# The second layer's Fourier projection, split into even and odd parts of its tokens and its channels

## Chip, core and metric

The kernel runs on one NeuronCore of one Trainium2 chip. The metric is the device time of one execution in microseconds (us). Three runs of the kernel before gave 2589.39, 2590.97 and 2591.15 us, so its median is 2590.97 us.

## What is computed

A two-layer encoder trunk over T = 272 tokens (16 meta tokens and 256 others) of width D = 2048, all in float32. Per layer:

```
h = RMSNorm(x)
[q | k | v | f | ga | gf] = h @ W_in
attention: 8 query heads, 2 key heads of 128, per-head RMSNorm, 2-D rotary, softmax over all 272 tokens
fourier:   for each of 8 groups of 128 channels of f: Re(FFT2 over tokens and channels), ortho
x = x + (sigmoid(ga) * (attn @ W_attn_br) + sigmoid(gf) * (fourier @ W_four)) @ W_out
x = x + W_down( silu(dwconv3(RMSNorm(x) @ W_up_gate)) * (RMSNorm(x) @ W_up_val) )
```

The real part of the 2-D transform is a cosine transform over tokens of a cosine transform over channels, less a sine transform of a sine transform. The cosine part sees only what is even in the tokens (x[n] + x[272-n]) and even in the channels (w[c] + w[128-c]), the sine part only what is odd in both.

## The kernel before

Everything is kept with channels on the 128 partitions and tokens along the free dimension. The residual stream XT is [128, 16, 272]; xH and xL are its two halves in fp32r after multiplication by the norm's weights (`norm_split`, L379), H the rounded value and L the rest. A product of two float32 numbers is three fp32r matmuls: H times H, H times L, L times H.

**Weights** are streamed in the order written down in the list `order` (from L117 on), in chunks of [128, 4, 256] float32 (512 KB). `advance` (L158) issues a chunk's load on SP's queue, four buffers deep (RAW = 4), and queues two tasks: for the weights of the Fourier branch, `fold_w` (L176), two VectorE instructions that make sums and differences of halves of the chunk (tile `wpm`); for every chunk `split_w` (L182), a ScalarE cast into `wh` and a VectorE subtraction into `wl` (three buffers each). `pump` (L169) issues these tasks between the matmuls, two chunks ahead (LOOK = 2).

**Groups.** `group` (L212) makes 256 output channels of one projection: over 16 input tiles it issues, for each of two halves m, the three matmuls of L240, L241 and L242 into one PSUM bank. Banks have two tags of four each, "mm" for the groups and "aux" for everything else. Where only 256 tokens are needed (the second layer's feed-forward), the first two matmuls become one of 512 columns (L236, L237). `four_group` (L256) does the same for the Fourier branch's output weights, on even and odd parts: one matmul of 276 columns (H and L of 138 tokens, L275), then one of 138 (L276).

**Side work** is written as generators: `push` puts one on the list `shadow`, and `step` (L197), called after every second of a chunk's eight weight tiles (four times a chunk, 16 times a group of four chunks), runs at most one that is due up to its next `yield n`, which makes it wait n steps. `drain` (L208) runs all of them to the end. What is written this way sets priorities; the framework's planner then fixes each engine's order of instructions at compile time, and lets an instruction that is ready in its plan pass one that is not. In the trace VectorE thus runs L847 of a second half ahead of L850 of the first.

**Order around the change.** Layer 0: f, k, v, four groups q, gates and branches, `o`, then the feed-forward: 22 pairs of groups `ug` and `uv` and 16 groups `d`, 264 chunks, with `norm_stats` (L397) at its start. Layer 1 begins with the four groups f (L553): each is 256 channels over all 272 tokens, `f_evac` (L449) multiplies by 1/rms and adds and subtracts mirrored tokens, and the generator `f_chan` (L463) makes the channel transform by float32 matmuls of 65 columns; after the fourth, `f_tok` (L498) makes the token transform. Then come k with `head_evac` and `kstats` (L607), v with `vtrans`, q with `q_stage` (L665), which releases `attend` (L692), the attention that runs beside the rest.

Of the kernel before, what the change touches and what calls it, by code (L numbers as in the profile page):

```python
# [10 lines left out]
F32 = mybir.dt.float32  # L11
F32R = mybir.dt.float32r
# [4 lines left out]
P = 128  # L17
# [17 lines left out]
FF_SPLIT = (24, 20)  # L35

# [66 lines left out]

def _rep(ap, n):
    return ap.unsqueeze(1).to_broadcast([ap.shape[0], n, ap.shape[1]])
# [3 lines left out]
def encoder_kernel(ctx, tc, xT, params, consts, bmat, w_in, w_abr, w_four, w_f64, w_out, w_up, w_down, outT):  # L109
# [3 lines left out]
    psum = ctx.enter_context(tc.tile_pool(name="psum", bufs=4, space=bass.MemoryType.PSUM))  # L113

# [3 lines left out]
    for l in range(DEPTH):  # L118
        def g(w, mg, k0, k1):
            return [(w[l, mg, c], CW) for c in range(k0 // CW, k1 // CW)]  # L120
        if l == 0:
            f01 = [g(w_in, IN_F + i, 0, KT) for i in range(2)]
            order.append(((l, "f01"), [ch for pr in zip(*f01) for ch in pr]))
        for i in range(2 if l == 0 else 0, 4):
            order.append(((l, "f", i), g(w_in, IN_F + i, 0, KT)))
# [270 lines left out]

    def norm_stats(holder):  # L397
# [26 lines left out]
    for l in range(DEPTH):  # L424
# [6 lines left out]
        with tc.tile_pool(name=f"mix{l}", bufs=1) as mp:  # L431
            E = mp.tile([P, NG, T], F32, tag="q1", name="E")
            AHn = 3 * 4 * T
            ALn = 2 * 4 * T
            o1Hf = mp.tile([P, AHn], F32R, tag="aH", name="o1H")
            o1Lf = mp.tile([P, ALn], F32R, tag="aL", name="o1L")
            o1H, o1L = (t_[:, :4 * 4 * HC].rearrange("p (i b c) -> p i b c", i=4, b=4) for t_ in (o1Hf, o1Lf))
# [4 lines left out]
            def rt(name):  # L442
                return mp.tile([P, 2, T], F32, tag="r", name=name, bufs=7)
# [18 lines left out]

            def f_chan(i):  # L463
# [6 lines left out]
                hh = o1H[:, i]  # L470
                nc.scalar.copy(hh, pv[:, :, 0:HC])
                nc.vector.tensor_tensor(o1L[:, i], pv[:, :, 0:HC], hh.bitcast(F32), op=ALU.subtract)
                for m in range(2):
                    h1 = o64[:, 0, 4 * m + i:4 * m + i + 1]
                    nc.scalar.copy(h1, pv[:, m, HC:HC1])
                    nc.vector.tensor_tensor(o64[:, 1, 4 * m + i:4 * m + i + 1], pv[:, m, HC:HC1], h1.bitcast(F32), op=ALU.subtract)
                if i == 3:
                    yield 1
# [16 lines left out]
                    yield from f_tok()  # L495
                yield 1

            def f_tok():  # L498
# [10 lines left out]
                for i in range(4):  # L509
                    pb = psum.tile([P, 512], F32, tag="aux", name="ps_fb")  # L510
                    pv = pb.rearrange("p (e n) -> p e n", e=2)[:, :, :TH]
                    for b in range(2):
                        oh, ol = (t_[:, i, 2 * b:2 * b + 2, :].rearrange("p m c -> p (m c)") for t_ in (o1H, o1L))
                        nc.tensor.matmul(pv[:, b, :], oh, BH[:, b, :], start=True, stop=False)
                        nc.tensor.matmul(pv[:, b, :], oh, BL[:, b, :], start=False, stop=False)
                        nc.tensor.matmul(pv[:, b, :], ol, BH[:, b, :], start=False, stop=False)
                        nc.tensor.matmul(pv[:, b, :], o1r[:, i, :], br3[:, b, :], start=False, stop=True)
                    nc.scalar.copy(fr[:, i, :, 0, :], pv)
                    nc.vector.tensor_tensor(fr[:, i, :, 1, :], pv, fr[:, i, :, 0, :].bitcast(F32), op=ALU.subtract)
                    yield 2  # L520

            if l == 0:
# [27 lines left out]
                nc.vector.tensor_scalar(bgh, prm[:, P_BG:P_BG + DEPTH * 2 * KT], 0.5, None, op0=ALU.mult)  # L550
            else:
# [47 lines left out]
            ps = group((l, "k", 0), xr(0), T)  # L599
            kp, ksq = head_evac(ps, prm[:, P_KN + l:P_KN + l + 1], "kp", 0)  # L600
# [6 lines left out]
            def kstats():  # L607
# [19 lines left out]
                rope(kp, qs, kH, kL)  # L627

            push(kstats(), 4)
# [9 lines left out]
            def vtrans():  # L639
                for kv in range(NKV):  # L640
# [12 lines left out]
                    yield 2  # L653

# [7 lines left out]
            qH = mp.tile([P, NH, T], F32R, tag="q1", name="qH")  # L662
            qL = mp.tile([P, NH, T], F32R, tag="q2", name="qL")
# [28 lines left out]
            def attend():  # L692
                for kv in range(NKV):
# [166 lines left out]
        with tc.tile_pool(name=f"ffn{l}", bufs=1) as fp:  # L860
            hold = {}
            push(norm_stats(hold), 8)
            fused = 2 * W2 <= 512
            k0 = 0
            for c, n in enumerate(FF_SPLIT):
                gHL = fp.tile([P, FF_SPLIT[0], 2, T], F32R, tag="gHL", name="gHL")
                gH, gL = gHL[:, :, 0, :], gHL[:, :, 1, :]
                for i in range(k0 // MG, (k0 + n) // MG):
                    ps = group((l, "ug", i), xr(lo), W)
                    drain()  # L870
# [45 lines left out]
                k0 += n  # L916

# [20 lines left out]

def _cols(a):
    return a.reshape(-1, P).T  # L940
# [27 lines left out]
```

## Time and profile before

| what | value |
|---|---|
| median of three runs | 2590.97 us |
| the profiled execution's own time | 2590.29 us |
| its span, first to last instruction | 2588.4 us |
| TensorE, share of the span | 100% (2577.4 us) |
| VectorE | 65% (1691.3 us) |
| ScalarE | 47% (1210.0 us) |
| DMA queue of SP | 457.37 MB, 51.6% of 16 engines |
| layer 1's groups f, first to last matmul | 1329.3 to 1380.9 us |
| layer 0's feed-forward, first ug to last d | 533.0 to 1329.2 us |

The profile is one execution. "Busy" is the share of the span in which an engine ran something; a matmul is pipelined and its end is modelled, so how fast TensorE gets on is read from the distance between the starts of two matmuls and not from their length. L numbers are lines of the kernel before. The clock granted to TensorE was 1.000 throughout.

### The profile page before, as it was taken

How to read it: one execution, taken by the hardware profiler on the slowest of the kernel's cores; microseconds unless marked ns; L12 is line 12 of the kernel's file. 1: busy time of each engine (PE TensorE's matmuls, PEld its weight loads, DVE VectorE, ACT ScalarE, POOL GpSimd, SP SyncE). 2: the span in 40 equal slices, each digit the busy share in tenths (PEclk: the TensorE clock that was granted, in tenths of full speed). 3: DMA queues.
4: the chain of work that ended last, by engine and by line, in shares of the span. 5: the costliest groups of instructions: out<-in, count | busy, mean ns of one | idle time of the engine just before them, and what ended most of it. 6: DMA issues, size and time to landing. Idle time of an engine off the chain costs nothing.

```text
span 2588.4 us, 47800 instructions
## 1 busy us (share of the span) xinstructions
PE 2577.4 (100%) x19706; PEld 2514.1 (97%) x19706; DVE 1691.3 (65%) x2689; ACT 1210.0 (47%) x1736; POOL 18.6 (1%) x38
## 2 busy tenths in 40 slices
PE   8999999999999999999999999999999999999999
PEld 8999999999999999999999999999999998899988
DVE  7687767766565445565556878677766665566654
ACT  5455434554444334444444555445544543354443
POOL 0000000000000000000000000000000000000000
PEclk9999999999999999999999999999999999999999
DMA  6544555545555555555544545555555555555554
GB/s 234 165 151 164 191 180 189 181 171 177 174 177 174 176 174 174 176 175 176 174 169 151 173 155 199 192 194 188 183 186 186 186 187 188 187 183 186 186 199 159
DMA packets 131995, 465.34 MB, mean 180 GB/s; under 512 B 15296, under 2 KB 19264, under 8 KB 131776
## 3 DMA queue, kind: packets, MB, share of 16 engines
q1 hardware_dynamic: 127408, 457.37, 51.6%
q10 hardware_dynamic: 4368, 4.92, 0.6%
q8 instruction: 154, 2.52, 0.4%
q14 instruction: 65, 0.53, 0.1%
HBM read 457.35 MB, written 2.10 MB: 178 GB/s over the span
## 4 chain that ended last, share of the span: by engine, by line
PE 97%; DVE 1%; DMA 1%; ACT 1%; issue 0%; SPq 0%; POOL 0%; DVEq 0%; ACTq 0%
PE ps_ug L241 7%; PE ps_ug L240 7%; PE ps_ug L242 7%; PE ps_uv L236 6%; PE ps_d L236 6%; PE ps_d L240 4%; PE ps_d L241 4%; PE ps_d L242 4%; PE ps_uv L240 3%; PE ps_uv L241 3%; PE ps_uv L242 3%; PE ps_uv L237 3%; PE ps_d L237 3%; PE ps_o L241 2%; PE ps_o L242 2%; PE ps_o L240 2%
## 5 line engine op out<-in xcount | busy, mean ns | idle before, releaser
L188 DVE TENSOR_TENSOR wl<-raw,wh 128x1024 fp32r<-128x1024 f32 (+1 forms) x834 | 1017.0, 1222 | 724.0 <-ACT wh L187 718.6
L187 ACT CAST wh<-raw 128x1024 fp32r<-128x1024 f32 (+1 forms) x834 | 871.6, 1047 | 1025.1 <-issue 168.7
L241 PE MATMUL ps_ug<-xHL,wh 128*128 128x272 f32 (+1 forms) x1408 | 402.4, 286 | 0.0
L240 PE MATMUL ps_ug<-xHL,wh 128*128 128x272 f32 (+1 forms) x1408 | 402.0, 285 | 0.0
L242 PE MATMUL ps_ug<-xHL,wl 128*128 128x272 f32 (+1 forms) x1408 | 401.8, 285 | 0.0
L240 PEld LDWEIGHTS ps_ug<-xHL,wh 128*128 128x128 f32 x1408 | 265.4, 188 | 1.0
L241 PEld LDWEIGHTS ps_ug<-xHL,wh 128*128 128x128 f32 x1408 | 265.5, 189 | 0.1
L242 PEld LDWEIGHTS ps_ug<-xHL,wl 128*128 128x128 f32 x1408 | 264.9, 188 | 0.0
L236 PE MATMUL ps_uv<-xHL,wh 128*128 128x512 f32 x704 | 247.7, 395 | 0.0
L236 PE MATMUL ps_d<-gHL,wh 128*128 128x512 f32 x664 | 233.1, 395 | 0.0
L241 PE MATMUL ps_d<-gHL,wh 128*128 128x272 f32 (+1 forms) x744 | 214.4, 288 | 0.0
L240 PE MATMUL ps_d<-gHL,wh 128*128 128x272 f32 (+1 forms) x744 | 214.1, 288 | 0.0
L242 PE MATMUL ps_d<-gHL,wl 128*128 128x272 f32 (+1 forms) x744 | 214.0, 288 | 0.0
L241 PE MATMUL ps_uv<-xHL,wh 128*128 128x272 f32 x704 | 203.1, 288 | 0.0
L240 PE MATMUL ps_uv<-xHL,wh 128*128 128x272 f32 x704 | 202.9, 288 | 0.0
L242 PE MATMUL ps_uv<-xHL,wl 128*128 128x272 f32 x704 | 202.7, 288 | 0.0
L237 PE MATMUL ps_uv<-xHL,wl 128*128 128x256 f32 x704 | 197.7, 281 | 0.0
L237 PE MATMUL ps_d<-gHL,wl 128*128 128x256 f32 x664 | 186.5, 281 | 0.0
L236 PEld LDWEIGHTS ps_uv<-xHL,wh 128*128 128x128 f32 x704 | 132.4, 188 | 29.9
L236 PEld LDWEIGHTS ps_d<-gHL,wh 128*128 128x128 f32 x664 | 125.0, 188 | 29.2
L240 PE MATMUL ps_ga<-xHL,wh 128*128 128x272 f32 (+1 forms) x512 | 148.2, 289 | 0.0
L240 PE MATMUL ps_gf<-xHL,wh 128*128 128x272 f32 (+1 forms) x512 | 147.1, 287 | 0.0
(273 smaller groups left out, 5899.6 us busy)
## 6 DMA issues: line engine op xcount, KB each, us to landing
raw<-in_w_up SPq DMA_DIRECT2D x352, 512.0 KB, 3.5
raw<-in_w_in SPq DMA_DIRECT2D x207, 512.0 KB, 3.6
raw<-in_w_down SPq DMA_DIRECT2D x176, 512.0 KB, 3.4
raw<-in_w_out SPq DMA_DIRECT2D x64, 512.0 KB, 3.5
raw<-in_w_four SPq DMA_DIRECT2D x32, 512.0 KB, 3.9
raw<-in_w_abr SPq DMA_DIRECT2D x32, 512.0 KB, 3.6
qs<-qp ACTq DMA_DIRECT2D x32, 68.0 KB, 3.8
outT<-ot ACTq DMA_DIRECT2D x16, 128.0 KB, 3.5
```

Of the source, the lines that this page charges most:

```text
L187: nc.scalar.copy(h[:, a:b], r[:, a:b])
L188: nc.vector.tensor_tensor(lo[:, a:b], r[:, a:b], h[:, a:b].bitcast(F32), op=ALU.subtract)
L236: nc.tensor.matmul(o2, h[:, c, sl], ab, start=kt == 0, stop=False)
L237: nc.tensor.matmul(o, lo[:, c, sl], ab[:, 0, :], start=False, stop=kt == nk - 1)
L240: nc.tensor.matmul(o, h[:, c, sl], a, start=kt == 0, stop=False)
L241: nc.tensor.matmul(o, h[:, c, sl], b, start=False, stop=False)
L242: nc.tensor.matmul(o, lo[:, c, sl], a, start=False, stop=kt == nk - 1)
```

## The change

Layer 1 no longer projects f from 272 tokens and 1024 channels. `fold_pair` makes the even and the odd part of the tokens (138 each) of two input tiles at a time, in fp32r halves, in eight slots; `folded_f` multiplies them by folded weights (64 even and 64 odd channels for each group; channel 64 of each of the eight groups is done apart, with 16 columns of weights w64s). Eight accumulators, four double groups by even and odd, fill the eight PSUM banks, so one pass over the 16 input tiles makes all of f. `folded_chan` takes the place of `f_chan`. The order in layer 1 becomes k, v, the first q group, f4, the other q groups.

The folded weights are made by `prefold` as side work of layer 0's feed-forward: 32 pieces of 512 KB (16 of the projection, 16 of the Fourier branch's output weights) are loaded, added and subtracted on VectorE, and stored into the DRAM tile `fw`; layer 1 loads its chunks for f4 and s from there, and `fold_w` is used in layer 0 alone. Waits for all side work (`drain`) become waits for one flag (`until`). `attend` waits for the end of `f_tok` and of `kstats`. The feed-forward ends with a `drain()`. In both layers, `vt` uses the buffer of qL, and qH and qL are claimed after the first q group.

```diff
+            if l == 1 and i == 0:
+                order.append(((l, "f4"), [(fw[kt], CW) for kt in range(KT)]))
         for half in range(2):
             for kind, j in BRANCH_ORDER[half]:
                 w, off, n = {"ga": (w_in, IN_GA, KT), "gf": (w_in, IN_GF, KT), "s": (w_four, 0, 8), "a": (w_abr, 0, 8)}[kind]
-                order.append(((l, kind, j), g(w, off + j, 0, n)))
+                chs = [(fw[KT + 2 * j + c], CW) for c in range(2)] if (l, kind) == (1, "s") else g(w, off + j, 0, n)
+                order.append(((l, kind, j), chs))
...
-    folded = {i for i, k in enumerate(k for k, chs in order for _ in chs) if k[1] == "s"}
+    folded = {i for i, k in enumerate(k for k, chs in order for _ in chs) if k[:2] == (0, "s")}
...
+    def until(hold, flag):
+        while flag not in hold:
+            step(True)
...
+    def prefold(pool):
+        src = [w_fl[k] for k in range(KT)] + [w_four[1, j, c] for j in range(NG) for c in range(2)]
+        ins, outs = {}, {}
+        for j in range(len(src) + 2):
+            if j < len(src):
+                ins[j] = pool.tile([P, CW, MG * P], F32, tag="pfi", name=f"pfi{j}", bufs=2)
+                nc.sync.dma_start(ins[j], src[j])
+            yield 2
+            if 0 <= j - 1 < len(src):
+                a, o = ins.pop(j - 1), pool.tile([P, CW, MG * P], F32, tag="pfo", name=f"pfo{j}", bufs=2)
+                half = (lambda t_, q: t_[:, :, q * P:(q + 1) * P]) if j - 1 < KT else (lambda t_, q: t_[:, 2 * q:2 * q + 2])
+                for q, op in ((0, ALU.add), (1, ALU.subtract)):
+                    nc.vector.tensor_tensor(half(o, q), half(a, 0), half(a, 1), op=op)
+                    yield 1
+                outs[j - 1] = o
+            yield 2
+            if j >= 2:
+                nc.sync.dma_start(fw[j - 2], outs.pop(j - 2))
...
                 push(norm_stats(hold), 8)
-                for i in range(3):
-                    ps = group((l, "f", i), xr(0), T)
-                    if i == 0:
-                        drain()
-                    f_evac(i, ps)
-            f_evac(3, group((l, "f", 3), xr(0), T))
-            tok, tok2 = hold["tok"], hold["tok2"]
+                nc.gpsimd.memset(remE, 0.0)
+                nc.gpsimd.memset(remO, 0.0)
...
+                nc.sync.dma_start(w64c, w_f64c)
...
+                nc.scalar.copy(w64s[:, :, 0:NG], w64c)
+                nc.vector.tensor_tensor(w64s[:, :, NG:], w64c, w64s[:, :, 0:NG].bitcast(F32), op=ALU.subtract)
+            NS, NA = 8, 5
...
+            def fold_pair(b, slots):
+                t1 = rt("t1")
+                nc.vector.tensor_tensor(t1, XT[:, 2 * b:2 * b + 2, :], bc2(rstdB), op=ALU.mult)
+                hf = rw("hf").rearrange("p k (e n) -> p k e n", e=2)
+                nc.vector.tensor_tensor(hf[:, :, 0, 1:TH], t1[:, :, 1:TH], t1[:, :, T - 1:T - TH:-1], op=ALU.add)
+                nc.scalar.copy(hf[:, :, 0, 0:T // 2 + 1:T // 2], t1[:, :, 0:T // 2 + 1:T // 2])
+                nc.vector.tensor_tensor(hf[:, :, 1, :], t1[:, :, 1:TH + 1], t1[:, :, T - 1:T - TH - 1:-1], op=ALU.subtract)
+                for q in range(2):
+                    k = 2 * b + q
+                    sl = slots[k % NS]
+                    gc = prm[:, P_NM + l * KT + k:P_NM + l * KT + k + 1]
+                    nc.scalar.activation(sl[:, :, 0, :], hf[:, q], AF.Copy, scale=gc)
+                    nc.vector.scalar_tensor_tensor(sl[:, :, 1, :], hf[:, q], gc, sl[:, :, 0, :].bitcast(F32),
+                                                   op0=ALU.mult, op1=ALU.subtract)
+            def fold_ahead(slots):
+                for b in range(NS // 2):
+                    fold_pair(b, slots)
+                    yield 2
+                hold["ahead"] = True
+            def folded_f(slots, E):
+                assert order[st["grp"]][0] == (l, "f4")
+                st["grp"] += 1
+                ps = {}
+                for g in (0, 1, 2, 3):
+                    ps[g] = [psum.tile([P, 512], F32, tag="aux" if g < 2 else "mm", name=f"ps_f{g}{e}") for e in range(2)]
+                p64 = ps[0][0][:2 * NG, 2 * TH:3 * TH]
+                for k in range(KT):
+                    i = st["next"]
+                    advance(i + 1 + LOOK)
+                    pump(i)
+                    h, lo_ = splits.pop(i)
+                    st["next"] += 1
+                    sl = slots[k % NS]
+                    for g in (0, 1, 2, 3):
+                        for e in range(2):
+                            w = slice(e * P, (e + 1) * P)
+                            o2 = ps[g][e][:, :2 * TH].rearrange("p (r n) -> p r n", r=2)
+                            nc.tensor.matmul(o2, h[:, g, w], sl[:, e], start=k == 0, stop=False)
+                            if g == e == 0:
+                                for r in range(2):
+                                    nc.tensor.matmul(p64, w64s[:, k, :], sl[:, 0, r, :], start=False, stop=False)
+                            nc.tensor.matmul(ps[g][e][:, :TH], lo_[:, g, w], sl[:, e, 0, :], start=False, stop=k == KT - 1)
+                        pump()
+                        if k == KT - 1:
+                            for e in range(2):
+                                nc.scalar.copy(E[:, g, e, :], ps[g][e][:, TH:2 * TH])
+                                nc.vector.tensor_tensor(E[:, g, e, :], ps[g][e][:, :TH], E[:, g, e, :], op=ALU.add)
+                            if g == 0:
+                                nc.scalar.copy(e64, p64)
+                    if k % 2 and k + NS < KT:
+                        fold_pair((k + NS - 1) // 2, slots)
...
+            def folded_chan(E):
+                cf = rw("cf").rearrange("p a b -> p (a b)")
+                nc.sync.dma_start(cf[:, :cfold.shape[1]], cfold)
+                sg = rw("sg").rearrange("p a b -> p (a b)")[:2 * NG, :CW * 2 * HC1]
+                nc.sync.dma_start(sg, csign)
...
+                yield 2
+                for i in range(4):
+                    pa = psum.tile([P, 512], F32, tag="aux", name="ps_fa")
+                    nc.tensor.matmul(pa[:, 0:n2], E[:, i, 0, 0:P], cct, start=True, stop=False)
+                    nc.tensor.matmul(pa[:, 0:n2], e64[:, 0:P], sg[:, i * n2:(i + 1) * n2], start=False, stop=True)
+                    nc.tensor.matmul(pa[:, n2:2 * n2], E[:, i, 1, 0:P], sct, start=True, stop=True)
+                    chan_out(i, pa[:, 0:4 * HC1].rearrange("p (b n) -> p b n", b=4))
+                    yield 2
...
+                pr = psum.tile([P, 512], F32, tag="aux", name="ps_fr")
+                nc.tensor.matmul(pr[:, :n2], remE.rearrange("p g n -> p (g n)"), cct, start=True, stop=False)
+                nc.tensor.matmul(pr[:, :n2], e64r.rearrange("p g n -> p (g n)"), sat[:2 * NG], start=False, stop=False)
+                nc.tensor.matmul(pr[:, :n2], remO.rearrange("p g n -> p (g n)"), sct, start=False, stop=True)
+                hold["fold"] = True
...
+                yield 5
+                yield from f_tok()
+                hold["ftok"] = True
...
             push(kstats(), 4)
+            if last:
+                slots = fold_setup()
+                push(fold_ahead(slots), 2)
 
             ps = group((l, "v", 0), xr(0), T)
-            drain()
-            vt = mp.tile([P, NKV, 3 * P], F32, tag="om", name="vt")
+            if last:
+                until(hold, "keys")
+            else:
+                drain()
+            vt = mp.tile([P, NKV, 3 * P], F32, tag="q2", name="vt")
...
             def attend():
+                while "ftok" not in hold or "keys" not in hold:
+                    yield 1
...
-                push(q_stage(i, *head_evac(ps, prm[:, P_QN + l:P_QN + l + 1], "qp", lo)), 4)
+                qq = head_evac(ps, prm[:, P_QN + l:P_QN + l + 1], "qp", lo)
+                if last and i == 0:
+                    until(hold, "vt")
+                    until(hold, "ahead")
+                    folded_f(slots, E)
+                    o1_tiles()
+                    push(folded_chan(E), 1)
+                    q0 = qq
+                    continue
+                if i == int(last):
+                    until(hold, "vt")
+                    until(hold, "fold")
+                    qH = mp.tile([P, NH, T], F32R, tag="q1", name="qH")
+                    qL = mp.tile([P, NH, T], F32R, tag="q2", name="qL")
+                    if last:
+                        push(q_stage(0, *q0), 1)
+                push(q_stage(i, *qq), 4)
...
+            if not last:
+                push(prefold(fp), 8)
...
-                    drain()
+                    until(hold, "tok2")
```

More of the change, by code (lines that the diff above doesn't have):

```diff
@@ L35 @@
 FF_SPLIT = (24, 20)
+F0 = 1536
 def _branch(text):
@@ L101, in _constants, with _consts_fold @@
     return np.ascontiguousarray(consts), np.ascontiguousarray(bmat)
+def _consts_fold():
+    j, c = np.arange(HC), np.arange(HC1)
+    cc = np.cos(2.0 * np.pi * ((j[:, None] * c[None, :]) % P) / P) / math.sqrt(P)
+    sc = np.sin(2.0 * np.pi * ((j[:, None] * c[None, :]) % P) / P) / math.sqrt(P)
+    sc[:, 0] = sc[:, HC] = 0.0
+    sc[0] = 0.0
+    two = lambda m: np.kron(np.eye(2), m)
+    sg = np.zeros((P, CW, 2, HC1))
+    sa = np.zeros((P, 2, HC1))
+    gq = np.zeros((P, CW))
+    gm = (np.arange(P)[:, None] // 32 == np.arange(CW)[None, :]).astype(np.float64)
+    for r in range(2 * NG):
+        g, m = r % NG // 2, r % 2
+        sg[r, g, m] = sa[r, m] = (-1.0) ** c / math.sqrt(P)
+        gq[r, g] = 1.0
+    a = np.concatenate([two(cc), two(sc), sa.reshape(P, -1), gq, gm], 1)
+    return np.ascontiguousarray(a.astype(np.float32)), np.ascontiguousarray(sg.reshape(P, -1)[:2 * NG].astype(np.float32))
 def _rep(ap, n):
@@ L123, in encoder_kernel @@
             order.append(((l, "f01"), [ch for pr in zip(*f01) for ch in pr]))
-        for i in range(2 if l == 0 else 0, 4):
-            order.append(((l, "f", i), g(w_in, IN_F + i, 0, KT)))
+            for i in range(2, 4):
+                order.append(((l, "f", i), g(w_in, IN_F + i, 0, KT)))
         order.append(((l, "k", 0), g(w_in, IN_K, 0, KT)))
@@ L469, in f_chan @@
                     nc.tensor.matmul(pv[:, 2 + m, :], E[:, gi, 128:256], scm, start=True, stop=True)
[L470 to L476, printed above, removed]
+                chan_out(i, pv)
                 if i == 3:
+                    hold["fold"] = True
                     yield 1
@@ new lines, in encoder_kernel, with fold_setup @@
+            NS, NA = 8, 5
+            def fold_setup():
+                hA = mp.tile([P, AHn], F32R, tag="aH", name="hA")
+                hB = mp.tile([P, ALn], F32R, tag="aL", name="hB")
+                slots = []
+                for k in range(NS):
+                    t_, q = (hA, k) if k < NA else (hB, k - NA)
+                    n = 4 * TH
+                    slots.append(t_[:, q * n:(q + 1) * n].rearrange("p (e r n) -> p e r n", e=2, r=2))
+                return slots
+            def fold_pair(b, slots):
[12 more added lines that the diff above has]
+                                                   op0=ALU.mult, op1=ALU.subtract)
@@ L653, in vtrans @@
                     yield 2
+                hold["vt"] = True
             push(vtrans(), 4)
@@ L936, in _four, with _fl @@
     return _tiles(wz[:, rows]), w64
+def _fl(w):
+    wz = np.concatenate([w, np.zeros((D, 1), w.dtype)], 1)
+    c = np.arange(HC)
+    cols = np.concatenate([np.concatenate([P * g + c if k == 0 else np.where(c == 0, NG * P, P * g + P - c)
+                                           for g in (2 * q, 2 * q + 1)]) for q in range(CW) for k in range(2)])
+    w_fl = np.ascontiguousarray(wz[:, cols].reshape(KT, P, CW, MG * P))
+    w64 = np.ascontiguousarray(w[:, P * np.arange(NG) + HC].reshape(KT, P, NG).transpose(1, 0, 2))
+    return w_fl, w64
 def _cols(a):
```

66 lines of the change are left out of this document (57 added, 9 removed).

## The prediction

> **What bounds the kernel now.** I read the page first, for the busy shares and the chain that ended last.
>
> ```profile
> span 2588.4 us, 47800 instructions
> PE 2577.4 (100%) x19706; PEld 2514.1 (97%) x19706; DVE 1691.3 (65%) x2689; ACT 1210.0 (47%) x1736; POOL 18.6 (1%) x38
> ...
> PE 97%; DVE 1%; DMA 1%; ACT 1%; issue 0%; SPq 0%; POOL 0%; DVEq 0%; ACTq 0%
> ```
>
> TensorE (PE) carries 97% of the chain, so what takes matmuls away counts in full, as long as nothing else falls behind it. How dense they are is seen in the timeline: three starts of the group f in layer 1, and the even and odd pairs of the Fourier branch, whose shapes (276, then 138 columns) are those of the new code.
>
> ```profile
> 1343.30 0.29 PE L240 MATMUL ps_f<-xHL,wh 128*128 128x272 f32 x1
> 1343.43 0.29 PE L241 MATMUL ps_f<-xHL,wh 128*128 128x272 f32 x1
> 1343.55 0.29 PE L242 MATMUL ps_f<-xHL,wl 128*128 128x272 f32 x1
> 1343.68 0.29 PE L240 MATMUL ps_f<-xHL,wh 128*128 128x272 f32 x1
> ...
> 1595.07 0.23 PE L276 MATMUL ps_s<-fr,wl 128*128 128x138 f32 x1
> 1595.13 0.28 PE L281 MATMUL ps_s<-x,w 96*128 96x138 f32 x1
> 1595.24 0.34 PE L275 MATMUL ps_s<-fr,wh 128*128 128x276 f32 x1
> 1595.42 0.23 PE L276 MATMUL ps_s<-fr,wl 128*128 128x138 f32 x1
> 1595.48 0.34 PE L275 MATMUL ps_s<-fr,wh 128*128 128x276 f32 x1
> 1595.65 0.23 PE L276 MATMUL ps_s<-fr,wl 128*128 128x138 f32 x1
> 1595.72 0.33 PE L275 MATMUL ps_s<-fr,wh 128*128 128x276 f32 x1
> ```
>
> Three matmuls of 272 columns take 0.377 us (13 such triples in a row: 4.90 us). A pair of 276 and 138 takes 0.24 us start to start, where 414 columns at the first rate would take 0.19: two loads of 128 columns of weights (PEld) seem to set it, about 0.12 each.
>
> Third, what is left beside TensorE: the stages' sums (columns: window; its length; busy time of PE, PEld, DVE, ACT, POOL; clock; DMA share; GB/s), then two groups of VectorE (DVE) and the landing time of a load.
>
> ```profile
> 12.00:16.00 4.00, 4.00 (x34) 4.00 (x33) 3.77 (x7) 3.83 (x8) 0.00 (x0) 1.00 1.03 419
> 533.00:684.00 151.00, 151.00 (x1204) 150.92 (x1203) 93.16 (x134) 70.10 (x92) 0.85 (x1) 1.00 0.50 175
> 1396.70:1412.10 15.40, 15.40 (x124) 15.24 (x123) 10.15 (x23) 4.66 (x8) 1.56 (x5) 1.00 0.35 115
> ...
> L188 DVE TENSOR_TENSOR wl<-raw,wh 128x1024 fp32r<-128x1024 f32 x831 | 1015.5, 1224 | 722.9 <-ACT wh L187 717.5 <-PE ps_s L281 2.1
> L179 DVE TENSOR_TENSOR wpm<-raw 128x512 f32<-128x512 f32 x64 | 42.0, 688 | 14.5 <-DMA raw<-in_w_four 13.7
> ...
> raw<-in_w_up SPq DMA_DIRECT2D x352, 512.0 KB, 3.5
> ```
>
> The reader should see that layer 0's feed-forward leaves VectorE 38% idle and the DMA engines half idle, and that the engines moved 419 GB/s in the busiest stretch, but 175 at a share of 0.50, which is 350 at a share of 1.
>
> **The change, part by part**, against the profiled execution (2588.4 us of span and 1.9 around it, 2590.29).
>
> 1. *The projection.* Removed: 4 groups x 16 tiles x 2 halves = 128 triples x 0.377 = 48.2 us. Added: 16 tiles x 8 pairs = 128 pairs; eight of them last from 1595.24 to 1597.15, so 128 x 0.239 = 30.6 us. For channel 64, 32 matmuls of 138 columns with 16 columns of weights come in, which no row shows. Lower end: only their columns count. 138 columns at the 272-column rate are 0.063; the pair that holds two of them is then 690 columns, 0.32 in place of 0.24, or 0.04 each: 1.2 us. Upper end: L281 with 128 columns of weights added 0.11, so 3.5. I take the middle, 2.4, as both rows are as far. Sum -15.2, from -16.4 to -14.1.
> The Trainium skill (TensorE: Matmul & The Clock Gate, LDWEIGHTS) says that a weight load takes as many ns as columns / 1.2, so 13 ns for 16 and 107 for 128; by it these matmuls would cost near the lower end and the term would be -16.4.
>
> 2. *The channel transform.* Four float32 matmuls of 65 columns took 0.81 us (1346.69 to 1347.50), four times. Now three of 130; the nearest row, 138 columns of float32 (L504), took 0.20, so 0.6. Four times -0.2, one matmul more in the remainder (+0.2): -0.6.
>
> 3. *Layer 1's `wpm`* (32 x 0.69 = 22 us of VectorE) goes. TensorE stalls before s groups now: starts lie 0.3 and 0.13 late at 1593.77 and 1597.15, 0.23 and 0.13 at 1615.68 and 1618.99. Gain 0 to 1.0, taken 0.8.
>
> 4. *The start of layer 1.* A pair of tiles costs VectorE 0.72 (544 columns, as L588) + 2 x 0.44 (L519) + 2 x 0.50 (L382) = 2.6 us, 2.2 where they queue (instructions start 0.09 sooner than the one ahead ends). Four pairs fall in the v group: 10.15 busy and 9 to 10 more in about 15 us, 4 to 5 too much. Two chunks of split weights, 6 us of matmuls, stand before a stall: 0 to 1.5, taken 0.7. In f4 a chunk lasts 2.06 us; two chunks of the first eight ask VectorE for 2 x 1.22 + 2.6 = 5.0 (4.4 queued) in 4.1: 4 x 0.3 to 4 x 0.9, and a chunk's split is now only 4 us ahead: 0 to 5, taken 2.3. ScalarE has 2 x 1.05 + 2 x 0.52 + 0.2 = 3.3 of 4.1. Then q1 needs "mm" banks that hold f4's last sums: the evacuation (0.27 on ScalarE, 0.30 on VectorE, L827 and L828) may stand behind a cast and a split (1.05, 1.22), while 0.5 us of matmuls cover it: 0.3 to 2.5, taken 1.2. Sum +4.2, from 0.3 to 9.
> Small or covered: w64c, the constants and the signs are three more loads on SP, some 0.3 MB, ahead of which weights lie four chunks deep; POOL has two memsets of 0.2 us and else idles. The attention waits for `f_tok`: by the steps, `rqs` of the first head pair comes in the 13th step of the third q group (12th before) and `f_tok` ends in its 11th, so `attend` starts one step later. It ended at 1543.6 and is needed at 1565.9. If it came 22 us later, it would cost what is over.
>
> 5. *The preparation in layer 0.* 200 steps, four to a chunk: 50 chunks, 151 us. VectorE: 64 additions x 0.69 = 44 us (38 queued) on top of 93: 87 to 91%. Layer 1's attention stage ran at 50.8 of 59.3 (86%) with TensorE idle 0.24. DMA: 64 x 0.524 + 50 x 0.524 = 59.8 MB. At 419 GB/s 143 us, covered; at 350, 171 us, 20 too many. Nothing here can gain. The row at full share is nearer to a stage that asks for 396 GB/s than the idle one: I take 1. The store of a piece is issued 2 steps, 1.5 us, before the addition two pieces on wants its buffer, and lands after 3.5 or more. The planner lets others pass by the landing time in its plan; what the chip takes longer, VectorE waits, with the splits behind it. It has 14 to 20 us to spare, about 0.5 per piece: cost 0 up to the 32 us of rival 1, taken 2. SP's queue gets 64 issues of 0.43 us, 27 of 151, beside 50 weight loads; a store waits for an addition a piece old. Sum +3.
>
> In all -15.2 - 0.6 - 0.8 + 4.2 + 3 = -9.4: 2580.9 for an execution like the profiled one, which lay 0.7 under the median of the runs, so 2581.6.
>
> **Rivals.**
> 1. *VectorE waits for the stores* in the preparation. For: two buffers; the queue holds a load or two of weights ahead of each store (1.27 us each at 419 GB/s). Against: slower matmuls thin the traffic out by themselves. With a wait of w per piece the price is 32 x (w - 0.5); from w = 0.9 on the change loses. At w = 1.2: 22 in place of 2, 2602. At w = 1.5, 32.
> 2. *The transfers saturate* below what the stage asks for, at 350 GB/s, a straight line through the 0.50 share. Against: the 419 row, though that holds loads alone. 20 in place of 1: 2600. The turn lies where the stage needs 11 us more, at 369 GB/s. The Trainium skill (DMA: Bandwidth & Descriptors, Where 436 GB/s comes from) says that HBM to SBUF is bound by HBM's share of one core, about 358 GB/s; by it the stage would need 167 us and the kernel 2596. Its page HBM Reference (Specifications) restricts this to both cores of a pair at work and puts a core alone at about 425, which the 419 of this trace bears out.
> 3. *VectorE falls behind at layer 1's start*: 9 in place of 4.2, 2586.5.
> 4. *All hides*: 1 us in place of the 7.2 of steps 4 and 5, 2575.5.
> 5. *The fold saves nothing*, as pairs run at the pace of weight loads: two loads in place of three already give 30.6; only a stall brings it to 48. I give this no chance.
>
> **How the numbers follow.** Forecast (2577 to 2586) 0.53; rival 1 0.17, rival 2 0.13, rival 3 0.09, rival 4 0.08. The range runs from rival 4 with the projection at its better end, 2574, to rival 1 at w = 1.3, 2606; what is left out, a wait longer than that above all, I put at 0.15. A difference under 0.2%, 5.2 us, can't be told from none here: faster is below 2585.8, with 0.53 + 0.08 and a little of rival 3, 0.63; slower above 2596.2, rivals 1 and 2 without their small ends, 0.25; the same 0.12.
>
> **What would show it.** Step 1: pairs of `ps_f` 0.24 apart and f4 in 33 us. Step 3: no gaps before layer 1's s groups. Step 4: starts of TensorE more than 0.1 us late in v and f4, VectorE full there. Step 5: layer 0's feed-forward, 796 us now, no more than 3 longer; DMA share near 1 in its first 150 us; idle time of VectorE before the additions put down to a DMA would speak for rival 1, full share and late `raw` for rival 2. The prediction is wrong if that stretch grows by over 8 us, or f4 takes over 38.

## The result and the profile after

The changed kernel takes 2610.63 us (median of six runs), the kernel before 2590.44 beside it: 1.0082 of its time, 95% interval 1.0069 to 1.0095. It is slower by 20 us, where 9 less were forecast and 2606 was the end of the range. The lines of its page that answer to those shown of before:

```profile
span 2608.3 us, 47795 instructions
PE 2578.4 (99%) x19604; PEld 2507.6 (96%) x19604; DVE 1719.6 (66%) x2742; ACT 1215.6 (47%) x1762; POOL 20.5 (1%) x40
...
fw<-pfo SPq DMA_DIRECT2D x32, 512.0 KB, 7.7
```

TensorE is as good as full again, so the page alone doesn't tell where 20 us went. Cut into stages, from the start of one group to the start of another, the two traces and those of the experiments give (us; "time" is the median for before, changed, e_spread, p_spread, p_both and p_swap and a single run for the others; the names are those of the experiments below, where each edit is told):

| kernel | layer 0's feed-forward | layer 1's start to its first ga | from there to its first ug | time |
|---|---|---|---|---|
| before | 796.3 | 133.0 | 374.3 | 2590.4 |
| changed | 821.2 | 127.9 | 373.6 | 2610.6 |
| e_noprep | 796.3 | 128.3 | 373.5 | 2585.2 |
| e_dveonly | 796.4 | 129.5 | 373.5 | 2586.7 |
| e_dmaonly | 800.6 | 128.1 | 373.6 | 2589.6 |
| e_bufs | 800.5 | 127.7 | 373.5 | 2589.3 |
| e_nostore | 802.3 | 127.6 | 373.5 | 2591.3 |
| e_in | 802.5 | 127.2 | 373.6 | 2592.1 |
| e_out | 801.0 | 129.3 | 373.6 | 2592.1 |
| e_poolq | 845.9 | 129.4 | 373.5 | 2636.8 |
| e_spread | 801.7 | 127.4 | 373.5 | 2592.7 |
| p_spread | 796.3 | 128.2 | 373.5 | 2586.3 |
| p_both | 796.3 | 134.5 | 375.2 | 2592.4 |
| p_swap | 796.3 | 123.6 | 375.7 | 2583.7 |
| e_not1 | 796.3 | 127.9 | 375.3 | 2588.3 |

So the stage that carries the preparation lost 24.9 us, and layer 1 up to its first ug, which was to gain 12, gained 5.8. In the first stage the preparation runs from 534 to 725 us. The sums of two of its stretches in the changed kernel (columns as before: window; length; busy time of PE, PEld, DVE, ACT, POOL; clock; DMA share; GB/s), then the longest waits of SP's queue (above the dots) and some of the engines, from 533 to 740 us (total, times, longest):

```profile
600.00:640.00 40.00, 37.78 (x296) 37.07 (x296) 29.68 (x47) 15.74 (x21) 0.00 (x0) 1.00 0.96 328
...
683.00:690.00 7.00, 6.60 (x28) 6.29 (x29) 5.57 (x9) 3.48 (x6) 0.00 (x0) 0.51 0.63 229
```

```profile
SPq L433 <- DVE pfo L439: 57.9, 17, 7.0
SPq L179 <- DVE wl L214: 29.5, 16, 3.6
SPq L433 <- DVE gHL L1101: 10.0, 2, 5.7
...
ACT wh L213 <- DMA raw<-in_w_up: 50.2, 22, 5.0
DVE wl L214 <- ACT wh L213: 34.9, 28, 3.6
...
DVE pfo L439 <- DMA fw<-pfo: 11.7, 9, 2.3
PE ps_uv L270 <- ACT wh L213: 8.1, 3, 2.9
```

TensorE itself stood idle for 15.2 us of this window, 10.0 of them for casts and 5.2 for splits. Two readings offer themselves. The DMA engines are near their full share at 328 GB/s, and the cast L213 waits for weights: the transfers saturate (rival 2). Or: SP's queue stands still, 90 us in all, at L433, the load of a piece, which waits for VectorE to free its buffer (57.9 of the 90 are put down to the additions by name); the weight loads L179 stand behind it. The timeline of SP shows how that looks:

```profile
637.36 0.33 SPq L433 DMA_DIRECT2D pfi<-in_w_four  x1
637.73 0.91 SPq L179 DMA_DIRECT2D raw<-in_w_up  x2
638.68 0.43 SPq L444 DMA_DIRECT2D fw<-pfo  x1
642.27 0.33 SPq L433 DMA_DIRECT2D pfi<-in_w_four  x1
642.64 0.49 SPq L179 DMA_DIRECT2D raw<-in_w_up  x1
643.17 0.57 SPq L444 DMA_DIRECT2D fw<-pfo  x1
649.15 0.33 SPq L433 DMA_DIRECT2D pfi<-in_w_four  x1
649.52 1.44 SPq L179 DMA_DIRECT2D raw<-in_w_up  x2
```

From 638.7 to 649.5 one load of weights was issued, where TensorE at full pace uses one in 3.0 us; six us later, behind the matmul of 655.8, TensorE stood for 2.84 us. What the load of 649.15 waited for is seen on VectorE:

```profile
644.84 1.23 DVE L214 TENSOR_TENSOR wl<-raw,wh 128x1024 fp32r<-128x1024 f32 x1 [2.60 <-ACT wh L213]
646.69 1.23 DVE L214 TENSOR_TENSOR wl<-raw,wh 128x1024 fp32r<-128x1024 f32 x1 [0.63 <-ACT wh L213]
647.84 1.29 DVE L439 TENSOR_TENSOR pfo<-pfi 128x512 f32<-128x512 f32 x2
```

The addition stood behind two splits, and these waited for casts of weights whose loads had been issued at 637.7 and 638.3, right behind the load of a piece at 637.36, which had itself waited for VectorE.

### The profile page after: what moved, and what is told of

Read it like the earlier page. It is cut to its first block, busy times and chain, and to the rows that moved or that the text cites. A ratio compares the mean times of both kernels' runs of the same rounds, so it can differ in the third digit from the quotient of the medians.

```text
span 2608.3 us, 47795 instructions
## 1 busy us (share of the span) xinstructions
PE 2578.4 (99%) x19604; PEld 2507.6 (96%) x19604; DVE 1719.6 (66%) x2742; ACT 1215.6 (47%) x1762; POOL 20.5 (1%) x40
## 5 line engine op out<-in xcount | busy, mean ns | idle before, releaser
L214 DVE TENSOR_TENSOR wl<-raw,wh 128x1024 fp32r<-128x1024 f32 (+1 forms) x850 | 1036.2, 1221 | 717.5 <-ACT wh L213 712.8
L213 ACT CAST wh<-raw 128x1024 fp32r<-128x1024 f32 (+1 forms) x850 | 887.8, 1047 | 1013.9 <-issue 152.8
```

Source lines behind the costliest of these rows:

```text
L213: nc.scalar.copy(h[:, a:b], r[:, a:b])
L214: nc.vector.tensor_tensor(lo[:, a:b], r[:, a:b], h[:, a:b].bitcast(F32), op=ALU.subtract)
```

## The experiments in layer 0

Theory 1 is the saturation, theory 2 that VectorE waits for stores (rival 1), theory 3 that VectorE has too much to do.

**No preparation (e_noprep).**

```diff
-                order.append(((l, "f4"), [(fw[kt], CW) for kt in range(KT)]))
+                order.append(((l, "f4"), [(w_fl[kt], CW) for kt in range(KT)]))
...
-                chs = [(fw[KT + 2 * j + c], CW) for c in range(2)] if (l, kind) == (1, "s") else g(w, off + j, 0, n)
+                chs = g(w, off + j, 0, n)
...
-            if not last:
-                push(prefold(fp), 8)
```

> The preparation is left out: no loads, additions or stores of folded weights in layer 0's feed-forward, and layer 1 reads the unfolded pieces, so the kernel leaves out the additions that fold the weights. All theories: layer 0's feed-forward (first up-projection matmul to the first matmul of layer 1) goes from 821 back to 796 to 797 us, the kernel to 2585 to 2587; layer 1 as in the changed kernel, 128.0 us from its start to its first attention gate. If the stretch stays above 805, the loss isn't the preparation's.

796.3 and 2585.2: all of the 24.9 us belongs to the preparation.

**More buffers (e_bufs).**

```diff
-                ins[j] = pool.tile(..., tag="pfi", name=f"pfi{j}", bufs=2)
+                ins[j] = pool.tile(..., tag="pfi", name=f"pfi{j}", bufs=3)
...
-                a, o = ins.pop(j - 1), pool.tile(..., tag="pfo", name=f"pfo{j}", bufs=2)
+                a, o = ins.pop(j - 1), pool.tile(..., tag="pfo", name=f"pfo{j}", bufs=4)
```

> Three buffers for loaded pieces and four for folded ones in place of two and two; the same transfers and additions. Theory 1 (the transfers saturate at about 350 GB/s): nothing changes, the feed-forward 816 to 824 us, the kernel 2606 to 2614. Theory 2 (VectorE waits for a store to free its buffer): the wait goes, the feed-forward 796 to 800, the kernel 2586 to 2590. Theory 3 (VectorE has too much work): as theory 1.

800.5. The same bytes pass, and 20.7 of the 24.9 us are gone. Theory 1 falls by a row of this run's own, the stretch in which the changed kernel moved 328 GB/s:

```profile
600.00:640.00 40.00, 40.00 (x321) 40.00 (x321) 32.84 (x48) 17.39 (x22) 0.00 (x0) 1.00 1.02 410
```

410 GB/s over 40 us, loads and stores mixed, with TensorE never idle. The Trainium skill (DMA: Bandwidth & Descriptors, Where 436 GB/s comes from) puts the bound between HBM and SBUF at about 358 for one core; this row is over it, and under the 425 or so that its page HBM Reference (Specifications) gives a core alone.

**Transfers alone (e_dmaonly), additions alone (e_dveonly), no stores (e_nostore).** In e_dmaonly a piece is stored as it was loaded, from four buffers:

```diff
-                ins[j] = pool.tile(..., tag="pfi", name=f"pfi{j}", bufs=2)
+                ins[j] = pool.tile(..., tag="pfi", name=f"pfi{j}", bufs=4)
...
-                a, o = ins.pop(j - 1), pool.tile(..., tag="pfo", name=f"pfo{j}", bufs=2)
+                a = o = ins.pop(j - 1)
...
-                    nc.vector.tensor_tensor(half(o, q), half(a, 0), half(a, 1), op=op)
```

In e_dveonly all additions read `one`, a piece that is loaded once, and nothing is stored:

```diff
-                nc.sync.dma_start(ins[j], src[j])
+                ins[j] = one
...
-            if j >= 2:
-                nc.sync.dma_start(fw[j - 2], outs.pop(j - 2))
```

In e_nostore only the stores are left out (the last two lines above). In both, layer 1 reads the unfolded pieces, as in e_noprep.

> The preparation's transfers alone: each piece is loaded and stored as it came (four buffers), and the 64 additions are left out. Theory 1: 59.8 MB at 350 GB/s need 171 us where the stage has 151, the feed-forward 814 to 822 us. Theories 2 and 3: VectorE has no addition to do and nothing waits for a buffer, the feed-forward 796 to 799.

> The preparation's additions alone: the 64 additions read one piece that is loaded once, nothing is stored, and layer 1 reads the unfolded pieces, so folded weights are left out. Theory 3: VectorE is still asked for 91% of the stage, the feed-forward 812 to 822 us. Theories 1 and 2: 796 to 798.

> The preparation without its stores: 32 loads and 64 additions stay, nothing is written back, and layer 1 reads the unfolded pieces, so folded weights are left out. The stage then asks for 114 less 32 transfers of 0.524 MB, 43 MB in 151 us, 285 GB/s. Theory 1 (saturation at about 350 GB/s) and theory 2 (waits for stores): the feed-forward 796 to 799 us. Theory 3 (VectorE's load): 812 to 822. If it lies at 802 or more with VectorE idle, loads alone are slowed well under 350 GB/s.

Additions alone cost 0.1 us: theory 3 falls. Transfers alone cost 4.3, well under theory 1's 18 to 26 and over the 0 to 3 of the others. Without stores, 802.3: a miss for theories 1 and 2, which both had 796 to 799, and for theory 3 with 812 to 822. Its SP queue still waits 43 us at L433, 35 of them for VectorE, so waiting there and a loss of 6 come with no store at all. Its longest stall of TensorE, 2.4 us, ends at 655.7 with VectorE full and the DMA engines nearly idle:

```profile
653.00:656.00 3.00, 0.81 (x6) 0.59 (x6) 3.00 (x7) 1.65 (x3) 0.00 (x0) 1.00 0.23 94
```

**The two pairs of buffers apart (e_in, e_out), and another queue (e_poolq).** This gave theory 4: SP's queue, held by loads that wait for their buffer. Three edits, each alone:

```diff
-                ins[j] = pool.tile(..., tag="pfi", name=f"pfi{j}", bufs=2)
+                ins[j] = pool.tile(..., tag="pfi", name=f"pfi{j}", bufs=4)
...
-                a, o = ins.pop(j - 1), pool.tile(..., tag="pfo", name=f"pfo{j}", bufs=2)
+                a, o = ins.pop(j - 1), pool.tile(..., tag="pfo", name=f"pfo{j}", bufs=4)
...
-                nc.sync.dma_start(ins[j], src[j])
+                nc.gpsimd.dma_start(ins[j], src[j])
```

> Four buffers for loaded pieces, two for folded ones as in the changed kernel. Theory 4: a load finds its buffer free, and SyncE's queue isn't held: the feed-forward 797 to 803 us. Theory 2: the stores' buffers are as they were: 815 to 822.

> Two buffers for loaded pieces as in the changed kernel, four for folded ones. Theory 2: no wait for a store, the feed-forward 796 to 801 us. Theory 4: the loads go on waiting at SyncE for the additions, 40 us or more as in the kernel without stores, which lost 6: 802 to 815, the less the sooner VectorE reaches the additions.

> The 32 loads of pieces are issued from GpSimd's queue in place of SyncE's; buffers, additions, stores and the order of the rest as in the changed kernel. Theory 4 (SyncE's queue: the load of a piece waits there until VectorE has added the piece that held its buffer, 90 us of the stage's first 200 in the changed kernel, and the weight loads stand behind it): nothing stands behind that wait any more, the feed-forward 797 to 803 us. Theory 2 (VectorE waits for a store to free its buffer, 11 us in the changed kernel, with the splits behind it): 815 to 822, as nothing is changed there.

802.5, 801.0 and 845.9. Four buffers for the loads are enough, as theory 4 had it and theory 2 had not; four buffers for the stores are enough as well, as theory 2 had it, though SP still waits 47 us at L433, 38 of them for VectorE. (In e_in it waits 50 us too, at the stores.) So neither wait alone makes the loss: either pair, opened, takes 19 to 20 of the 25 us. And the move of the loads to GpSimd's queue, which theory 4 expected to help and theory 2 to change nothing, costs another 25. Its waits from 533 to 740 us:

```profile
SPq L444 <- DVE pfo L439: 58.5, 24, 6.6
...
POOL pfi L433 <- DVE pfo L439: 138.7, 29, 8.7
...
DVE pfo L439 <- DMA pfi<-in_w_four: 27.3, 9, 5.4
DVE pfo L439 <- DMA pfi<-in_w_fl: 21.6, 9, 5.2
...
PE ps_uv L272 <- DVE wl L214: 17.8, 7, 4.0
```

The wait of the loads now stands where no weights are behind it, and SP is held by the next one in line, a store that waits for its addition; VectorE stands 49 us before additions for their loads (0.4 in the changed kernel), with splits behind it. What fits all of these is a circle: a load waits on one in-order queue for an addition, the addition on another in-order queue for a store to land or behind a split for its weights, and the weights and splits that both queues also carry come late, which makes the additions late. Two buffers on both sides close it. One turn of it, by way of the weights, stands in the rows from 637 to 649 us above; that it makes up the whole loss was reasoned from the waits. That at this rate both pairs have to be short for the 20 us is what the runs show. The loss doesn't go by the length of SP's waits for pieces: some 43 to 50 us in e_dmaonly, e_nostore, e_in and e_out and 13 in e_bufs come with a loss of 4 to 6.

e_poolq lost its time elsewhere. TensorE stood idle for 30 us, all of them for splits and none for casts, and its clock was 0.92 on average from 534 to 740 us, 17 us of that stretch: 47 of the 50 us that it takes more than e_noprep. Why GpSimd's queue makes the additions wait so much for their loads was not followed further.

**A slower preparation (e_spread, p_spread).** First only the pauses were made five times as long (`yield 2` to 10, `yield 1` to 5).

> The same preparation at a fifth of the rate: every pause between its steps is five times as long, so that it takes 1000 of the stage's 1056 steps, some 755 us, in place of 151. It asks for 250 loads of weights, 32 loads and 32 stores of 0.524 MB, 165 MB in 755 us, 218 GB/s. Theory 1: nothing is late, the feed-forward 796 to 798 us, the kernel 2584 to 2588, faster than before by 0.1 to 0.25%. Theory 2: a store has 7.6 us to land in place of 1.5, against 7.7 of landing time, so no or little wait: 796 to 800. If each piece has a cost of its own at any rate (a queue held up, VectorE late), the stretch stays above 805.

2592.74, 1.0010 of before (1.0001 to 1.0019), 801.7 in the stage. The expectation failed because the preparation wasn't slowed to the 755 us meant: the pauses set priorities alone, and the planner moved the loads ahead, to between 534 and 739 us, as it seems whenever a buffer was free in its plan. The last addition started at 752.7 us, 212 after the first, where the changed kernel took 186. With the same two and two buffers this pace, with the order that the planner made of it, took 19.5 of the 24.9 us away, though VectorE stood longer for stores than in any run so far. Its waits and SP's from 533 to 1336 us:

```profile
DVE pfo L439 <- DMA fw<-pfo: 43.6, 26, 3.1
...
SPq L433 <- DVE pfo L439: 10.6, 7, 3.4
```

44 us of waiting for stores on VectorE, then, come with a loss of 5.4 in all, where 12 came with 24.9 in the changed kernel; what had gone was the wait of SP's loads, 11 us in place of 90. In the second run the long pauses stay and a load is tied into SP's queue behind a weight load, by an edge that orders issues and waits for nothing:

```diff
-        nc.sync.dma_start(r, src)
+        st["last"] = nc.sync.dma_start(r, src)
...
-                nc.sync.dma_start(ins[j], src[j])
+                with tc.issue_after(st["last"].ins):
+                    nc.sync.dma_start(ins[j], src[j])
```

> Pauses five times as long, as in the earlier run, and this time each load of a piece is put in SyncE's queue behind the weight load that the program issued last before it, so that the planner can't move it ahead: one piece comes to about eight weight loads. Theory 4: SyncE isn't held, weights are early, and the stage asks for about 218 GB/s: the feed-forward 796 to 798 us, the kernel 2583 to 2587, faster than before by 0.15 to 0.3%. If the four to six us that were left in the runs with more buffers belong to the preparation at any rate, 800 to 803.

2586.32: 0.9981 of before (0.9971 to 0.9990), and 796.3 in the stage, as without a preparation. First e_spread, then p_spread, in the same columns, and from p_spread's page the stores' landing time (the last number, us):

```profile
534.00:734.00 200.00, 197.06 (x1551) 196.10 (x1550) 150.26 (x227) 89.31 (x118) 1.22 (x1) 0.99 0.93 320
734.00:934.00 200.00, 200.00 (x1595) 200.00 (x1594) 108.87 (x134) 79.90 (x92) 0.00 (x0) 1.00 0.60 193
```

```profile
534.00:734.00 200.00, 200.00 (x1594) 199.92 (x1593) 133.03 (x194) 92.27 (x120) 0.85 (x1) 1.00 0.68 222
734.00:934.00 200.00, 200.00 (x1595) 200.00 (x1595) 114.72 (x144) 80.16 (x91) 0.00 (x0) 1.00 0.66 221
```

```profile
fw<-pfo SPq DMA_DIRECT2D x32, 512.0 KB, 3.7
```

With two buffers on each side and 222 GB/s in place of 320, nothing is late. At this rate the preparation costs nothing; so its rate against its buffers was the matter. Of the 24.9 us, 19 to 20 go with the short buffers. The other 4 to 6 stay in every run that moves pieces at the full rate, the one without additions (e_dmaonly) and the one whose loads never hold SP (e_bufs) among them, and are gone with transfers taken away or spread. They come with the transfers, then, but not plainly by late weights: TensorE's idle time there, 2.6 us in e_bufs, 2.8 in e_out and 4.8 in e_nostore, is put down to splits and none of it to casts. By which step the transfers, or the order that the planner gives VectorE with them, make these splits late wasn't settled.

## The experiments at layer 1's start

In the changed kernel f4 stalls for 3.4 us and the last three query groups for 3.3. ScalarE in the latter:

```profile
1466.45 0.40 ACT L745 ACTIVATE qps<-ps_q 128x258 f32<-128x258 f32 x1
1468.85 3.53 ACTq L759 DMA_DIRECT2D qs<-qp  x4
1472.40 1.28 ACT L913 ACT_TABLE_LOAD   x1 [5.56 <-issue]
...
1474.27 1.04 ACT L213 CAST wh<-raw 128x1024 fp32r<-128x1024 f32 x1
...
1477.82 0.39 PE L272 MATMUL ps_q<-xHL,wl 128*128 128x258 f32 x1 [1.71 <-DVE wl L214]
```

Four issues of the swapping transfers and a table load keep casts away from 1466.9 to 1474.3, and TensorE waits for the split behind them. (`qs` holds the swapped rows of a query pair.) Two edits on p_spread, first together, then the first alone:

```diff
-                    nc.scalar.dma_start(qs[32 * b:32 * b + 32, :, :], hp[...])
+                    nc.sync.dma_start(qs[32 * b:32 * b + 32, :, :], hp[...])
...
-                nc.vector.tensor_tensor(t1, XT[:, 2 * b:2 * b + 2, :], bc2(rstdB), op=ALU.mult)
+                nc.gpsimd.tensor_tensor(t1, XT[:, 2 * b:2 * b + 2, :], bc2(rstdB), op=ALU.mult)
```

> As the run before it, and two edits at layer 1's start: the four swapping transfers of a query pair are issued from SyncE in place of ScalarE, and the multiplication of a tile pair by the norm's factor runs on GpSimd in place of VectorE. If f4's 3 us of stalls come from VectorE being full, and the last query group's 3 from ScalarE's queue, in which the four issues stand ahead of a cast, the stretch from layer 1's start to its first attention gate goes from 128 to 122 to 124 us and the kernel to 2578 to 2582. If GpSimd takes over 2.5 us for a pair's product, the pairs come late: 126 to 132.

> The paced preparation, and of the two edits at layer 1's start only the one that issues the swapping transfers from SyncE; the multiplication is back on VectorE. In the run with both, the last three query groups took 48.0 us in place of 50.9. If that belongs to the swaps: the stretch from layer 1's start to its first attention gate 125 to 126 us in place of 128.2, the kernel 2582.5 to 2585, faster than before by 0.2 to 0.35%; the v group back from 20.5 to 13.4 us. If the stretch behind the gate, 375.2 us there and 373.5 elsewhere, stays long, the swaps cost that, and the gain is 1 us.

With both, 2592.44, and 134.5 in the stretch: worse than the 126 to 132 for a slow GpSimd, though its product took 1.6 us (mean of eight) and not over 2.5. The timeline of p_both shows why, GpSimd first:

```profile
1342.98 2.69 POOL L643 TENSOR_TENSOR t<-XT,rstdB 128x544 f32<-128x544 f32 x2 [2.46 <-ACT rstdB L467]
1344.39 1.59 DVE L645 TENSOR_TENSOR hf<-t 128x274 f32<-128x274 f32 x1 [0.95 <-POOL t L643]
1345.90 0.43 DVE L647 TENSOR_TENSOR hf<-t 128x276 f32<-128x276 f32 x1
...
1346.48 1.43 POOL L643 TENSOR_TENSOR t<-XT,rstdB 128x544 f32<-128x544 f32 x1 [0.80 <-DVE hf L647]
1346.61 1.60 DVE L647 TENSOR_TENSOR hf<-t 128x276 f32<-128x276 f32 x1
```

L645 and L647 take 0.43 us, and 1.6 when GpSimd's product runs beside them: VectorE is blocked about as long as the product lasts, so what was taken from it comes back as time blocked. The clock added to it: it was halved for 10.2 us of this stretch in p_both and for 3.4 in p_spread, which makes 3.4 of the 6.3 us between them. The Trainium skill (SBUF — State Buffer, SBUF: two separate sides) says that the two share a pair of ports, which whoever starts first holds alone for a whole instruction, VectorE's with two inputs from SBUF among them; these rows agree.

The swaps alone give 2583.67: 0.9972 of before (0.9961 to 0.9983), the fastest version here, 7 us ahead of the kernel before and 27 of the changed one. The stretch went from 128.2 to 123.6 (f4 36.4 in place of 38.4, the last three query groups 48.2 in place of 50.9); 2.2 came back behind the gate, 375.7 in place of 373.5, where TensorE now stands 1.64 and 0.72 us in the first ga group.

To test whether VectorE's load holds f4, the pairs' product was left out of p_swap (e_not1).

```diff
-                t1 = rt("t1")
-                nc.vector.tensor_tensor(t1, XT[:, 2 * b:2 * b + 2, :], bc2(rstdB), op=ALU.mult)
+                t1 = XT[:, 2 * b:2 * b + 2, :]
```

> As the run before it without the multiplication of the eight tile pairs by the norm's factor, 8 x 0.72 us of VectorE, which this run leaves out of the computation. If VectorE's load is what holds TensorE up in f4, its stalls go from 3.4 us to under 1.5, f4 from 38.4 to 35.5 to 37 us. If the handover of banks or the transfers hold it, f4 stays at 38 to 39.

f4 took 39.7 us, more than either guess, and nearer to the handover's. The rows don't let it rest there: VectorE, then TensorE, then a window behind the stall.

```profile
1371.88 0.49 DVE L746 SCALAR_TENSOR_TENSOR qp<-ps_q,prm,rstdB 128x258 f32<-128x258 f32 x1
...
1373.35 1.22 DVE L214 TENSOR_TENSOR wl<-raw,wh 128x1024 fp32r<-128x1024 f32 x1
1374.49 0.48 DVE L746 SCALAR_TENSOR_TENSOR qp<-ps_q,prm,rstdB 128x258 f32<-128x258 f32 x1
...
1375.02 0.40 PE L679 MATMUL ps_f<-hA,wh 128*128 128x276 f32 x1 [1.49 <-DVE qp L746]
```

```profile
1375.10:1382.50 7.40, 7.40 (x37) 7.29 (x38) 3.28 (x4) 2.95 (x4) 0.00 (x0) 0.54 0.41 143
```

The second evacuation of the first query group came behind three additions and a split, and f4 wanted its bank: 1.6 us, and then the clock was 0.54 for 7.4 us, 7.4 x 0.46 = 3.4 more. Less these two f4 would be 34.7. So an order of VectorE's queue that this edit changed hides what the lighter load gives; how the 3 us of f4 divide between load and handover is open.

## Why the prediction was wrong, by its steps

**Step 1, the projection (-15.2)**, was right: a pair takes 0.239 us, and 0.415 with the two matmuls for channel 64, 0.088 for each, so 30.6 + 2.8 in place of 48.2, -14.8. 0.088 lies between its bounds, 0.04 and 0.11, nearer to the upper one. Rival 5 didn't come.

**Step 2, the channel transform (-0.6)**, was mis-sized: counted from the first of a series to the next projection matmul, the twelve matmuls of 130 columns take 4.0 us in all, 0.33 each where the row of L504, a matmul that stands alone, had promised 0.20. That is 0.8 more than before; with 0.6 for the remainder +1.4.

**Step 3 (-0.8)** was right: 374.3 became 373.6 from the first ga on, and the two gaps within the s groups (0.30 and 0.23) are gone.

**Step 4, the start of layer 1 (+4.2, bounds 0.3 and 9)**, cost 8.3 by what is left of the balance (-5.1 = -14.8 + 1.4 + 8.3), near what rival 3 gave for it (9). Of the stalls it named, f4 has 3.4 us; v, where VectorE was busy 13.37 of 13.40 us, has 0.3 at most. What it lacked are the query groups behind f4: it priced there the handover of banks alone, and ScalarE's queue, with four DMA issues and a table load between two casts, cost most of 3.3 us (2.7 came back in p_swap). Some 1.6 us of the 8.3 are not traced.

**Step 5, the preparation (+3)**, is the failed step: +24.9. Its two terms fared unlike. The DMA term took the 419 row over 350 and 1 us; the choice of row was right (410 measured), and at most the 4 to 6 us that short buffers don't explain are its own. The store's term, 2 us, broke: 19 to 20 us go with the short buffers. It counted the wait on VectorE's queue alone and gave it 0.5 us a piece to spare, and took SP's queue as 64 issues by 0.43; that a piece's load waits at SP for its buffer, with all weights behind it, wasn't priced at all: 90 us of waiting, and 15 us in which TensorE stood idle, two thirds of them for casts of late weights. It also put the landing of a store at "3.5 or more", which is 3.7 in a quiet stage (p_spread) and was 7.7 in this one.

The forecast's own signs came as it wrote them: the stage grew by more than 8 us, f4 took 38.5. But "full share and late `raw` for rival 2" was a bad sign. Both were there, and the transfers were not at their limit. Rival 1 named the right pair of culprits, store and addition, and its w = 1.2 came within 9 us, but by the wrong queue, and that is luck: VectorE stood 11.7 us for stores, 0.4 a piece, for which its formula gives nothing; in e_spread it stood 1.4 a piece, for which the formula gives 28 us, and the stage lost 5.4.

## What to carry to other kernels

Before a load-work-store loop is put beside a stream on the same queue, follow each buffer round: which instruction frees it, on which in-order queue it waits, and what stands behind it there; a wait costs what is behind it, not what it lasts. A high DMA share with late loads is no proof of saturation: look at what the issuing queue did in the gap, and give the loop a buffer more before believing it. And to slow side work down, order it in the queue that issues it; longer pauses in the program leave the planner free to pull it together again.

## What was not expected of the hardware

TensorE's clock halved after some short stalls: in the changed kernel after 2.84 us at 655.8 and 3.10 us at 680.2 (0.51 from 683 to 690, shown above), but not after 2.61 us at 715.3; in e_not1 after 1.6 us; in e_out from 1378.4 to 1385.2 after three stalls in f4, the longest 0.9 us, which f4 of the changed kernel has as well, at full clock; and in e_bufs not after 3.1 us at 1455.4. The length of one stall doesn't decide it, then. In the preparation of the changed kernel, 49 steps of 0.1 us too much add up to 5 of the 24.9 us. The Trainium skill (TensorE: Matmul & The Clock Gate, HAM oscillation — how this bites in real kernels) sets the limit at idle gaps of about 3.4 us; the 1.6 here is under that, and the clock halved all the same. And a share near 1 goes with very unlike rates: 328 at 0.96 in the changed kernel, 410 at 1.02 with more buffers, in the same stretch.
